# Moving the triangular substitution of a gated DeltaNet layer from SBUF into two PSUM banks

## The chip, the cores and the metric

The kernel runs on one core of a Trainium2 chip. TensorE (PE) multiplies 128 x 128 tiles out of SBUF into PSUM, which has eight banks of 512 float32 columns in 128 partitions; VectorE (DVE), ScalarE (ACT) and GpSimd (POOL) do the elementwise work, and DMA queues are issued from SyncE (SP) and ScalarE. Each engine takes its own instructions in the order of the program and waits for the others on semaphores. The metric is the device time of one execution in microseconds (us); lower is better.

## What is computed

A two-layer encoder trunk over 1024 frames of 1024 features, float32: chunked softmax attention, an MLP, a gated DeltaNet layer, an MLP, a final norm. The change lies in the DeltaNet layer (8 heads of 128). Its core, cut from the reference:

```python
qkv = silu(causal_conv(h @ w_in[:, :3072], conv_w))      # 4 taps; q and k are l2-normalised afterwards
decay = exp(where(incl, gc[..., :, None] - gc[..., None, :], -inf))
L = where(strict, einsum('bhnid,bhnjd->bhnij', k * beta, k) * decay, 0.0)
M = L + eye(CHUNK)
sol = triangular_solve(M, rhs, lower=True, unit_diagonal=True)
...
def step(state, inp):                                    # scan over the chunks of a head
    v_new = u_c - einsum('bhck,bhkv->bhcv', w_c, state)
    o_c = einsum('bhck,bhkv->bhcv', qd_c, state) + einsum('bhij,bhjv->bhiv', qk_c, v_new)
    state = state * gl_c + einsum('bhck,bhcv->bhkv', kd_c, v_new)
    return state, o_c
```

## The kernel before

The kernel computes in chunks of 128 frames, so a head has 8 chunks. Dense products are made with weights and activations split into a high and a low float32r part, three products of 512 columns for each 128 x 128 weight tile; one output tile of 512 columns takes 24 of them and one PSUM bank.

In the DeltaNet stage (`deltanet` and `dn_run`) TensorE works through a list of dense jobs: k for all eight heads, then q, v and z in turn, then the first two panels of the output projection. Everything else is written as generators (tasks). After each dense product `turn` lets those tasks go one step whose priority and whose modelled engine load allow it, so their instructions are woven between the dense products. A model of time (`Clock`) decides in Python which step comes when: it charges an elementwise operation on VectorE about 0.08 us plus its elements at 960 per us, wherever its operands lie. The order that results is the program; on the chip each engine keeps to its own part of it. `Ring` objects model buffers with the modelled time at which each comes free; `sleep` leaves a modelled time for a load, `until` waits for a mark of another task.

The tasks that matter here:

- `dn_evac`: reads a dense bank (`acc`) on VectorE into `xp`, does the four-tap convolution on ScalarE, VectorE and GpSimd with buffers `cy` and `cz`, and writes k, q or v with a Silu on ScalarE. For the k of heads in `POOLED` (4 to 7) one of the additions is made by GpSimd (`cz <- cy, cz`) with a third ScalarE activation; otherwise VectorE makes two scalar_tensor_tensor operations.
- `dn_blocks`: products of k with itself, multiplied by the decays (`U`); the diagonal 32 x 32 blocks go to DRAM (`ud`).
- `dn_solves`: inverts the 32 x 32 diagonal triangles for four heads at a time, so twice (`g` = 0 and 1; "block 1" and "block 2" below), with one triangle in each partition. `fu` is the triangle, scaled with the inverse norms `rt`, which a TensorE transpose and four VectorE copies also spread into `rk`. `Z` (tile `fz`) starts as the identity. 31 steps follow, each a product into `tmp` (tile `ft`) and an addition into `Z`, both tensor_tensor operations on VectorE. `Z` is stored to DRAM as `zd`, and, transposed by ScalarE, as `xd`.
- `dn_inverse`: loads `zd` and `xd` back in another layout (`Zh`, `X`) and puts the inverse of the 128 x 128 triangle together on TensorE.
- `dn_prep_keys`, `dn_prep_queries`, `dn_prep_values`: the other operands, with products through the two `tp` banks.
- `dn_scans`: two lanes (even heads, odd heads) that run the scan over 8 chunks with small products into the PSUM tiles `s1` (two 128 x 128 results) and `s2` (the new state); ScalarE reads the output of a chunk out of `s1` into `o`. Head 0 may begin as soon as its operands are there; the second lane's head 1 waits for block 2.
- `dn_outs`: norm and gate.

PSUM in this stage has two banks for dense results (`acc`), two for `tp`, two for `s1` and two for `s2`. The inner loop of the substitution:

```python
for j in range(31):
    t = tmp[:, : (j + 1) * (31 - j)] ...
    right = Z[:, 0 : j + 1, j + 1 :]
    nc.vector.tensor_tensor(t, Z[:, 0 : j + 1, j : j + 1].broadcast_to(shape), fu[...], ALU.mult)
    nc.vector.tensor_tensor(right, right, t, ALU.add)
    yield
```

In the profile the engine calls of this stage all carry one line, L163 (the wrapper that meters them), so its instructions are told apart by their tiles: `acc`, `xp`, `cy`, `cz`, `fz`, `ft`, `fu`, `tp`, `s` (both scan tiles), `o`.

Of the kernel before, what the change touches and what calls it, by code (L numbers as in the profile page):

```python
# [7 lines left out]
F32 = mybir.dt.float32  # L8
F32R = mybir.dt.float32r
I32 = mybir.dt.int32  # L10
AF = mybir.ActivationFunctionType
ALU = mybir.AluOpType
AX = mybir.AxisListType
PSUM = bass.MemoryType.PSUM
DRAM = bass.MemoryType.DRAM

P = 128
# [3 lines left out]
HB = 512  # L21
# [13 lines left out]
ATT = (3, 2, 0.5, 1, 1, 0.7, 0.6)  # L35
RINGS = {"pt": 2, "po": 2, "sp": 1, "pr": 6, "bias": 3, "thi": 4, "tlo": 3, "oh": 1, "ot": 2}
ENGINES = {"dn_solves": ("vector",), "dn_decays": ("scalar",)}
POOLED = (4, 5, 6, 7)


def wide(col, p, n):
# [4 lines left out]
class Paced:  # L46


    def __init__(self, gens, slots):
        self.gens, self.slots = list(gens), slots  # L50
        self.total, self.done, self.at, self.n = sum(n for _, n in gens), 0, 0, len(gens)
# [13 lines left out]
    def drop(self, first=None):  # L65

        left = 0 if first is None else self.n - first
        while len(self.gens) > left:
            self.step()
# [116 lines left out]
class Ring:  # L186
# [9 lines left out]
    def take(self):  # L196
        if len(self.held) == self.n:
            self.held.pop(0)
        self.held.append([self.new(), None])
        return self.held[-1][0]  # L200

    def give(self, tile, t):
        for h in self.held:
            if h[0] is tile:
                h[1] = t


class Trunk:
# [961 lines left out]
    def up(self, i, ops, ap, mp, pp, gr, gt, finish, A, second, first, tail):  # L1170
# [21 lines left out]
        for n in range(last + 1):  # L1192
# [5 lines left out]
            X = self.bank()  # L1198
            Y, Z = (pp.tile([P, HB], F32, name=self.nm(z), tag=z) for z in "yz")

# [11 lines left out]
            def beside(bit, *steps):  # L1212

                if (G["u_first"] if n == 0 else G["u_second"] if n == 1 else G["u_last"] if n == last else G["u_other"]) >> bit & 1:
                    steps = steps[::-1]
                for step in steps:
                    step()

            def copied(k, ps):
                keep[k] = copy(ps)  # L1220

            def add(k, ps):
                nc.vector.tensor_tensor(keep[k], ps, keep[k], ALU.add)
# [3 lines left out]
            if n == 0:  # L1227
# [9 lines left out]
                next(finish)  # L1237
                self.block_product(Z, A["s1"], ops["t1"], True, True)
                copied("z5", Z)
                add("u2", Z)  # L1240
                R = next(finish)
# [12 lines left out]
            else:  # L1254
                next(sums, None)
                self.block_product(Z, A["s1"], ops["t1"], True, False)
                next(rest, None)
                beside(1, lambda: next(more, None), lambda: copied("z5", Z))
                next(sums, None)
# [414 lines left out]
    def deltanet(self, rhs, finish):  # L1674

        tc = self.tc
        with ExitStack() as es:
            self.tpp = es.enter_context(tc.tile_pool(name="tp", bufs=2, space=PSUM))
            self.sc = es.enter_context(tc.tile_pool(name="sc", bufs=2, space=PSUM))

            self.dq = es.enter_context(tc.tile_pool(name="dq", bufs=1))
            self.d1 = es.enter_context(tc.tile_pool(name="d1", bufs=1))
            self.db = es.enter_context(tc.tile_pool(name="db", bufs=2))
            self.drhs, self.finish = rhs, finish
            self.aux = lambda: self.tpp.tile([P, HB], F32, name=self.nm("tp"), tag="tp")
            rings = {
                "tp": Ring(2, self.aux), "acc": Ring(2, self.bank), "nt": Ring(3, self.nt),
                "s1": Ring(2, lambda: self.sc.tile([P, 2, P], F32, name=self.nm("s1"), tag="s1")),
                "s2": Ring(2, lambda: self.sc.tile([P, P], F32, name=self.nm("s2"), tag="s2"))}
            for t, n in (("xp", 2), ("cy", 2), ("cz", 2)):  # L1690
                rings[t] = Ring(n, lambda t=t, n=n: self.db.tile([P, 64 + HB], F32, name=self.nm(t), tag=t, bufs=n))
            self.begin(rings)
            self.silu_at, self.ready_at, self.solved = 0.0, set(), {}
            return self.timed(self.dn_run)
# [22 lines left out]
    def add(self, priority, steps):  # L1717


        self.tasks.append(Task(priority, steps))  # L1720
        self.tasks.sort(key=lambda t: t.priority)
# [12 lines left out]
    def idle(self):  # L1734

        now = self.clock.now
        self.turn()
        if self.clock.now == now:
            self.clock.at["tensor"] += 0.1
            self.idled += 0.1  # L1740
# [326 lines left out]
    def dn_evac(self, c, h, half, ps):  # L2067
# [17 lines left out]
        else:  # L2085
# [15 lines left out]
            yield  # L2101
            if c == "k" and h in POOLED:
                nc.gpsimd.tensor_tensor(z, y, z, ALU.add)
# [78 lines left out]
    def dn_solves(self):  # L2182

        nc, db = self.nc, self.db
        for g in range(2):
            fu = (self.dq, db)[g].tile([P, 32, 32], F32, name=self.nm("fu"), tag=("kbg", "zT")[g])
            Z = db.tile([P, 32, 32], F32, name=self.nm("fz"), tag="o")
            nc.gpsimd.memset(Z, 0.0)
            nc.gpsimd.memset(Z.rearrange("p c i -> p (c i)")[:, 0 : 32 * 32 : 33], 1.0)
            yield from self.until("u", 4 * g + 3)  # L2190
            nc.sync.dma_start(fu, self.ud[g])
            nb = self.sm.tile([P, 32], F32, name=self.nm("fnb"), tag="fnb")
            v = self.sm.tile([P, 32], F32, name=self.nm("frt"), tag="frt")
            for b in range(4):
                nc.sync.dma_start(
                    nb[32 * b : 32 * b + 32], self.grows[1][32 * g : 32 * g + 32, 32 * b : 32 * b + 32])
            yield from self.sleep(G["sl_solve"])

            diag = fu.rearrange("p j i -> p (j i)")[:, 0 : 32 * 32 : 33]
            nc.vector.tensor_scalar(v, diag, EPS, None, ALU.add)  # L2200
            yield
            yield from self.rsqrt_few(v, 32, "k")
            rt = self.got
            tp = yield from self.take("tp")
            nc.tensor.transpose(tp[:32, :P], rt, self.ident)
            yield
            for b in range(4):
                nc.vector.tensor_copy(
                    self.rk[32 * b : 32 * b + 32, 4 * g : 4 * g + 4].rearrange("p h q -> p (h q)"),
                    tp[:32, 32 * b : 32 * b + 32])  # L2210
            self.give("tp", tp)
            self.mark("rk", g)
            yield
            nc.vector.tensor_tensor(nb, nb, rt, ALU.mult)
            nc.vector.tensor_tensor(
                fu, fu, nb.rearrange("p (o i) -> p o i", o=1).broadcast_to([P, 32, 32]), ALU.mult)
            yield
            nc.vector.tensor_tensor(
                fu, fu, rt.rearrange("p (j o) -> p j o", o=1).broadcast_to([P, 32, 32]), ALU.mult)
            yield  # L2220
            tmp = self.np.tile([P, S], F32, name=self.nm("ft"), tag="ssum")
            for j in range(31):
                shape = [P, j + 1, 31 - j]
                t = tmp[:, : (j + 1) * (31 - j)].rearrange("p (c i) -> p c i", c=j + 1)
                right = Z[:, 0 : j + 1, j + 1 :]
                nc.vector.tensor_tensor(
                    t, Z[:, 0 : j + 1, j : j + 1].broadcast_to(shape), fu[:, j : j + 1, j + 1 :].broadcast_to(shape),
                    ALU.mult)
                nc.vector.tensor_tensor(right, right, t, ALU.add)
                yield  # L2230
            zd = self.dr.tile([P, 32, 32], F32, name=self.nm("zd"))
            xd = self.dr.tile([P, 32, 32], F32, name=self.nm("xd"))
            nc.sync.dma_start(zd, Z)
            X = tmp.rearrange("p (i c) -> p i c", c=32)
            for i in range(2):
                r = slice(16 * i, 16 * i + 16)
                nc.scalar.activation(X[:, r], Z[:, :, r].rearrange("p c i -> p i c"), AF.Copy)
                yield
            nc.scalar.dma_start(xd, X)
            self.solved[g] = zd, xd  # L2240
            self.mark("solve", g)
            yield

    def dn_inverse(self, h):
# [432 lines left out]
```

## Time and profile before

| | before |
|---|---|
| three timed runs | 2543.84, 2547.47, 2551.03 us; median 2547.47 |
| profiled execution | 2544.29 us, span 2542.5 us |
| mean granted TensorE clock | 0.989 of full speed |
| DeltaNet stage in the span | about 1190 to 1820 us |
| substitution, block 1 | 1311.5 to 1370.9 us |
| substitution, block 2 | 1401.8 to 1472.3 us |

The profile counts as busy the time in which an engine executes instructions; the products of TensorE overlap, so a busy TensorE is not necessarily at its peak. Rows that begin with a pair of times such as `1296.00:1382.00` are windows of the span: length, busy time and number of instructions of each engine, granted clock (PEclk), DMA share, GB/s. Rows of a group of instructions give busy time, mean duration in ns, and the idle time of the engine in front of them. A row `A <- B: 7.7, 3, 3.5` says that A waited for B 7.7 us in all, 3 times, at most 3.5 us. A row of the timeline gives start and duration.

### The profile page before, as it was taken

The page shows a single profiled execution, that of the slowest core. Times are in us where ns is not written, and L with a number is a line of the kernel's source. Part 1 is how long each engine was busy: PE and PEld are TensorE (multiplying, and loading weights), DVE is VectorE, ACT ScalarE, POOL GpSimd, SP SyncE. Part 2 cuts the span into 40 slices and gives each one's busy share as a digit, 9 for nine tenths or more (in the row PEclk, how much of TensorE's full clock was granted, in tenths as well). Part 3 has the DMA queues.
Part 4 walks back from the last instruction along what each step waited for, and adds up shares of the span by engine and source line. Part 5 has one row for each costly group of instructions (what it writes and reads, how often), then busy time and mean ns, then how long its engine had stood idle before and what let it go on. Part 6 is the DMA issues. An engine that isn't in the chain of part 4 may idle for free.

```text
span 2542.5 us, 36609 instructions
## 1 busy us (share of the span) xinstructions
PE 2455.7 (97%) x12750; PEld 2047.0 (81%) x12750; DVE 1786.7 (70%) x3058; ACT 1195.2 (47%) x2219; POOL 1287.8 (51%) x1088
## 2 busy tenths in 40 slices
PE   8999999999999999998888999999999999999997
PEld 6888888787888887886777888888787888887886
DVE  6666556678777688887578864444578777678887
ACT  6666667535555433334565333333335555433323
POOL 2444445614666566666474333433414756466655
PEclk9999999999999999999999999999999999999998
DMA  4222223423555977753354221222424555967752
GB/s 159 70 65 72 77 78 115 152 95 141 213 201 211 336 240 265 240 177 116 126 178 131 63 87 66 65 94 86 160 87 145 211 213 200 343 244 253 249 171 83
DMA packets 192760, 398.94 MB, mean 157 GB/s; under 512 B 53232, under 2 KB 59696, under 8 KB 192576
## 3 DMA queue, kind: packets, MB, share of 16 engines
q1 hardware_dynamic: 173136, 352.54, 41.2%
q10 hardware_dynamic: 19440, 44.07, 4.5%
q8 instruction: 100, 1.64, 0.3%
q14 instruction: 84, 0.69, 0.1%
HBM read 257.43 MB, written 130.71 MB: 153 GB/s over the span
## 4 chain that ended last, share of the span: by engine, by line
PE 66%; DVE 8%; issue 2%; DMA 2%; ACT 2%; SPq 1%; POOL 0%; ACTq 0%; DVEq 0%; POOLq 0%
PE y L1013 26%; PE z L1013 12%; PE acc L163 9%; PE acc L1013 7%; PE tp L163 5%; PE s L163 2%; PE acc L277 2%; PE acc L278 2%; PE acc L279 2%; DVE ft L163 1%; DVE fz L163 1%; DVE x L1518 1%; DMA vT<-grows 0%; DVE xs L394 0%; DVE cz L163 0%
## 5 line engine op out<-in xcount | busy, mean ns | idle before, releaser
L163 PE MATMUL acc<-xs,whi 128*128 128x512 f32 x1808 | 632.2, 413 | 13.2 <-DVE xp L163 7.7
L163 PEld LDWEIGHTS acc<-xs,whi 128*128 128x128 f32 x1808 | 335.8, 192 | 69.0 <-issue 4.1
L163 PE MATMUL acc<-xs,wlo 128*128 128x512 f32 x896 | 367.4, 410 | 1.6 <-POOL wlo L163 1.6
L1013 PE MATMUL y<-xs,whi 128*128 128x512 f32 x1008 | 311.7, 390 | 5.2 <-DVE x L1518 1.8
L163 POOL TENSOR_TENSOR wlo<-wraw,whi 128x512 fp32r<-128x512 f32 x126 | 165.8, 1316 | 223.6 <-ACT whi L163 196.0
L1028 POOL TENSOR_TENSOR s<-wraw 128x256 f32<-128x256 f32 (+1 forms) x93 | 92.0, 989 | 350.1 <-DVE a L1019 170.3
L1013 PEld LDWEIGHTS y<-xs,whi 128*128 128x128 f32 x1008 | 188.9, 188 | 47.3 <-DVE x L1518 2.6
L1019 DVE TENSOR_TENSOR wlo<-wraw,whi 128x512 fp32r<-128x512 f32 (+1 forms) x182 | 208.1, 1143 | 25.5 <-ACT whi L1022 25.5
L1022 ACT ACTIVATE whi<-wraw 128x512 fp32r<-128x512 f32 (+2 forms) x191 | 146.4, 767 | 120.4 <-PE y L1013 82.6
L1013 PE MATMUL y<-xs,wlo 128*128 128x512 f32 x504 | 196.4, 390 | 0.1
L1022 ACT ACTIVATE a<-s 128x256 fp32r<-128x256 f32 x122 | 63.8, 524 | 279.9 <-PE y L1013 137.4
L163 PEld LDWEIGHTS acc<-xs,wlo 128*128 128x128 f32 x896 | 172.0, 192 | 28.0 <-POOL wlo L163 2.4
L1013 PE MATMUL y<-xs,a 128*128 128x512 f32 x732 | 187.9, 392 | 6.4 <-DVE x L1518 6.4
L1518 DVE TENSOR_TENSOR x<-y,x 128x512 f32<-128x512 f32 x240 | 165.0, 688 | 34.6 <-PE y L1013 26.7
L1013 PEld LDWEIGHTS y<-xs,a 128*128 128x128 f32 x732 | 136.0, 188 | 40.0 <-DVE x L1518 10.2
L1013 PE MATMUL y<-xs,ahi 128*128 128x512 f32 x512 | 158.7, 391 | 7.7 <-ACT nt L1207 7.7
L1013 PE MATMUL acc<-xs,whi 128*128 128x512 f32 x528 | 162.9, 390 | 0.0
L163 POOL TENSOR_SCALAR pr<-pr,rs 128x640 f32<-128x640 f32 (+4 forms) x128 | 88.1, 691 | 129.4 <-DVE rs L163 98.2
L1013 PE MATMUL z<-xs,whi 128*128 128x512 f32 x480 | 147.9, 389 | 0.0
L163 POOL TENSOR_TENSOR cy<-cy,cz 128x512 f32<-128x512 f32 x48 | 63.0, 1313 | 166.8 <-DVE cz L163 106.6
L1095 DVE TENSOR_TENSOR c<-c 128x512 fp32r<-128x512 f32 x112 | 117.8, 1056 | 31.8 <-POOL c L1025 28.4
L163 DVE CUSTOM_DVE_ANT_0 pr<-sp,bias 128x640 f32<-128x640 f32 (+4 forms) x128 | 83.8, 655 | 64.0 <-PE sp L163 63.0
(351 smaller groups left out, 6087.0 us busy)
## 6 DMA issues: line engine op xcount, KB each, us to landing
xs<-gt SPq DMA_DIRECT2D x256, 256.0 KB, 4.8
gt<-c SPq DMA_DIRECT2D x112, 512.0 KB, 2.9
wraw<-in_w_up_dram SPq DMA_DIRECT2D x64, 512.0 KB, 3.7
wraw<-in_w_down_dram SPq DMA_DIRECT2D x64, 512.0 KB, 4.5
r<-gr SPq DMA_DIRECT2D x88, 256.0 KB, 3.6
wraw<-in_w_in_dram SPq DMA_DIRECT2D x32, 512.0 KB, 3.9
gr<-ssum ACTq DMA_DIRECT2D x62, 256.0 KB, 3.2
wraw<-in_w_qkv_dram SPq DMA_DIRECT2D x30, 512.0 KB, 3.4
```

Source lines behind the costliest of these rows:

```text
L163: return call(*args, **more)
L277: nc.tensor.matmul(ps, hi[:, k], xh, start=(k == 0), stop=False)
L278: nc.tensor.matmul(ps, hi[:, k], xl, start=False, stop=False)
L279: nc.tensor.matmul(ps, lo[:, k], xh, start=False, stop=(k == KT - 1))
L1013: nc.tensor.matmul(ps, w[:, k], x, start=bool(first and f), stop=bool(last and e), skip_group_check=True)
L1019: self.nc.vector.tensor_tensor(lo, src, hi.bitcast(F32), ALU.subtract)
L1022: self.nc.scalar.activation(hi, src, AF.Copy)
L1028: self.nc.gpsimd.tensor_tensor(out, x, y, ALU.add)
L1095: nc.vector.tensor_tensor(t[z][:, HB:].bitcast(F32R), t[z][:, HB:], t[z][:, :HB], ALU.subtract)
L1518: nc.vector.tensor_tensor(x, ps, x, ALU.add)
```

## The change

- The PSUM pool of the scans has one bank for `s1` and one for `s2`, and a tile `zz` of two banks.
- Until block 1 begins, the second bank of `zz` is a third bank for dense results (class `Spare`; `drop` takes it away once it is idle).
- `Z` is `zz`. It is filled by VectorE instead of GpSimd, after the loads of `fu` have been issued; the 9 us of `sl_solve` are counted from the same point as before.
- `rk` is written by one VectorE transpose of 32 x 32 blocks instead of a TensorE transpose and four copies.
- At the end ScalarE copies `zz` into an SBUF tile `F` (`fz`), and ScalarE's queue stores it; before, SP's queue stored `Z`. The transposed copies read `zz`.
- After block 2 the two banks become the second `s1` and `s2`.
- `POOLED` is empty.

```diff
-POOLED = (4, 5, 6, 7)
+POOLED = ()
...
+class Spare(Ring):
+    def __init__(self, n, new, spare=None):
+        super().__init__(n + (spare is not None), new)
+        self.spare = spare
+
+    def take(self):
+        spare = self.spare is not None and len(self.held) == self.n - 1
+        if len(self.held) == self.n:
+            spare = self.held.pop(0)[0] is self.spare
+        self.held.append([self.spare if spare else self.new(), None])
+        return self.held[-1][0]
+
+    def idle(self, now):
+        return all(t is not None and t <= now for x, t in self.held if x is self.spare)
+
+    def drop(self):
+        self.held = [x for x in self.held if x[0] is not self.spare]
+        self.n -= 1
+        self.spare = None
+
+    def add(self, spare):
+        self.n += 1
+        self.spare = spare
...
-            self.sc = es.enter_context(tc.tile_pool(name="sc", bufs=2, space=PSUM))
+            self.sc = es.enter_context(tc.tile_pool(name="sc", bufs=1, space=PSUM))
+            self.zz = self.sc.tile([P, 2, HB], F32, name="zz")
...
-                "tp": Ring(2, self.aux), "acc": Ring(2, self.bank), "nt": Ring(3, self.nt),
-                "s1": Ring(2, lambda: self.sc.tile([P, 2, P], F32, name=self.nm("s1"), tag="s1")),
-                "s2": Ring(2, lambda: self.sc.tile([P, P], F32, name=self.nm("s2"), tag="s2"))}
+                "tp": Ring(2, self.aux), "acc": Spare(2, self.bank, self.zz[:, 1]), "nt": Ring(3, self.nt),
+                "s1": Spare(1, lambda: self.sc.tile([P, 2, P], F32, name=self.nm("s1"), tag="s1")),
+                "s2": Spare(1, lambda: self.sc.tile([P, P], F32, name=self.nm("s2"), tag="s2"))}
...  (dn_solves)
-            Z = db.tile([P, 32, 32], F32, name=self.nm("fz"), tag="o")
-            nc.gpsimd.memset(Z, 0.0)
-            nc.gpsimd.memset(Z.rearrange("p c i -> p (c i)")[:, 0 : 32 * 32 : 33], 1.0)
+            zz = self.zz.rearrange("p b n -> p (b n)")
+            Z = zz.rearrange("p (c i) -> p c i", i=32)
...
-            yield from self.sleep(G["sl_solve"])
+            begin = self.clock.now
+            if g == 0:
+                while not self.rings["acc"].idle(self.clock.now):
+                    yield
+                self.rings["acc"].drop()
+            nc.vector.memset(zz, 0.0)
+            nc.vector.memset(zz[:, 0 : 32 * 32 : 33], 1.0)
+            yield
+            yield from self.sleep(begin + G["sl_solve"] - self.clock.now)
...
-            tp = yield from self.take("tp")
-            nc.tensor.transpose(tp[:32, :P], rt, self.ident)
-            yield
-            for b in range(4):
-                nc.vector.tensor_copy(
-                    self.rk[32 * b : 32 * b + 32, 4 * g : 4 * g + 4].rearrange("p h q -> p (h q)"),
-                    tp[:32, 32 * b : 32 * b + 32])
-            self.give("tp", tp)
+            nc.vector.transpose(self.rk[:, 4 * g : 4 * g + 4].rearrange("p h q -> p (h q)"), rt)
...
-            nc.sync.dma_start(zd, Z)
+            F = db.tile([P, 2, HB], F32, name=self.nm("fz"), tag="o")
+            for i in range(2):
+                nc.scalar.activation(F[:, i], self.zz[:, i], AF.Copy)
+                yield
+            nc.scalar.dma_start(zd, F.rearrange("p b (c i) -> p (b c) i", i=32))
...
             self.mark("solve", g)
+            if g:
+                self.rings["s1"].add(self.zz[:, 0, : 2 * P].rearrange("p (n t) -> p n t", t=P))
+                self.rings["s2"].add(self.zz[:, 1, :P])
             yield
```

## The prediction

> **What bounds the kernel now.** I read the page first: engine shares, then the slices with the granted clock.
>
> ```profile
> span 2542.5 us, 36609 instructions
> PE 2455.7 (97%) x12750; PEld 2047.0 (81%) x12750; DVE 1786.7 (70%) x3058; ACT 1195.2 (47%) x2219; POOL 1287.8 (51%) x1088
> ```
>
> TensorE is busy 97% of the span, so this change can only return time in which TensorE stands still, or runs at a lowered clock, in the DeltaNet stage. I cut that stage into windows to see how much there is.
>
> ```profile
> core 0: us, PE busy (x) PEld busy (x) DVE busy (x) ACT busy (x) POOL busy (x), PEclk, DMA share, GB/s
> 1214.00:1296.00 82.00, 76.30 (x355) 62.49 (x356) 44.20 (x92) 53.06 (x93) 42.67 (x32) 0.96 0.48 152
> 1296.00:1382.00 86.00, 69.65 (x346) 56.07 (x345) 79.14 (x130) 48.37 (x88) 49.88 (x41) 0.92 0.45 142
> 1382.00:1400.00 18.00, 18.00 (x154) 14.57 (x154) 13.48 (x32) 8.13 (x16) 6.97 (x7) 1.00 0.52 160
> 1400.00:1484.00 84.00, 79.96 (x682) 67.63 (x680) 71.99 (x147) 29.82 (x59) 28.75 (x23) 0.96 0.20 62
> 1484.00:1800.00 316.00, 314.34 (x2182) 271.07 (x2181) 157.09 (x361) 114.31 (x228) 114.83 (x84) 0.99 0.27 87
> ```
>
> A window loses its length less PE busy, and on top of that (1 - PEclk) of its length. From 1296 to 1382, where the first substitution runs, that is 16.4 us idle and 0.08 x 86 = 6.9 us of clock: 23.2 us. From 1400 to 1484, the second substitution: 4.0 and 3.4, so 7.4 us. From 1214 to 1296: 5.7 and 3.3, so 9.0 us. Behind 1484 TensorE is idle for only 1.7 us of 316. VectorE fills 79.14 of 86 us in the worst window; the chain of waits says whose work that is, and the waits of TensorE say what it stood for.
>
> ```profile
> by line: DVE ft L163 20.5%; DVE fz L163 19.4%; issue 12.8%; DVE cz L163 6.3%; DVE xp L163 5.9%; DMA vT<-grows 5.5%; DVE U L163 5.1%; DMA xd<-ft 3.8%; PE acc L163 2.9%; DVE fu L163 2.7%; DVE cy L163 2.5%; PE tp L163 2.5%; DMA X<-xd 2.3%; ACT
> PE acc L163 <- DVE xp L163: 7.7, 3, 3.5
> PE tp L163 <- ACT nt L163: 3.2, 2, 2.2
> PE tp L163 <- ACT k L163: 2.8, 2, 1.7
> PE tp L163 <- DMA X<-xd: 1.3, 2, 0.9
> ```
>
> In this window (all five rows are for 1296 to 1382) 40% of the chain is the substitution's two operations, `ft` (product) and `fz` (addition). TensorE waits 7.7 us for `xp`, the reading of a dense bank, which queues behind them on VectorE.
>
> **The change, part by part.** (a) *Z in PSUM.* Each block runs 31 steps of two tensor_tensor operations on (j+1)(31-j) elements, 5456 elements in all for each of the two. What they take, block 1 and then block 2:
>
> ```profile
> L163 DVE TENSOR_TENSOR fz<-fz,ft 128x31 f32<-128x31 f32 (+15 forms) x31 | 24.3, 784 | 1.1
> L163 DVE TENSOR_TENSOR ft<-fz,fu 128x31 f32<-128x31 f32 (+15 forms) x31 | 19.3, 624 | 0.5
> L163 DVE TENSOR_TENSOR ft<-fz,fu 128x31 f32<-128x31 f32 (+15 forms) x31 | 20.7, 668 | 0.2
> L163 DVE TENSOR_TENSOR fz<-fz,ft 128x31 f32<-128x31 f32 (+15 forms) x31 | 17.1, 551 | 1.1
> ```
>
> So 43.6 and 37.8 us. The timeline shows what undisturbed ones take, and what disturbs them:
>
> ```profile
> 1341.35 0.43 DVE L163 TENSOR_TENSOR fz<-fz,ft 128x256 f32<-128x256 f32 x1
> 1401.75 0.19 DVE L163 TENSOR_TENSOR ft<-fz,fu 128x31 f32<-128x31 f32 x1
> ...
> 1460.38 1.04 POOL L163 TENSOR_TENSOR ub<-ub,rk 64x512 f32<-64x512 f32 x1
> 1460.50 4.16 DVE L163 TENSOR_TENSOR ft<-fz,fu 128x112 f32<-128x112 f32 x1
> 1461.39 1.89 POOL L163 TENSOR_TENSOR dc<-dc,rk 128x1024 f32<-128x1024 f32 x1
> 1463.24 1.28 POOL L163 TENSOR_TENSOR wlo<-wraw,whi 128x512 fp32r<-128x512 f32 x1
> 1464.69 0.27 DVE L163 TENSOR_TENSOR fz<-fz,ft 128x112 f32<-128x112 f32 x1
> ```
>
> 0.43 us for 256 elements and 0.19 for 31 give 0.155 us plus 1/960 us an element. Hence 62 x 0.155 + 2 x 5456/960 = 21.0 us a block undisturbed: 22.6 and 16.8 us are stretching. The `ft` of 112 elements that lasted 4.16 us began inside one GpSimd operation and ended with the third of a row of them; its twin took 0.27. Is it the two SBUF inputs? Operations of this stage with one input in PSUM, and ones with both in SBUF (ns, min/median/max):
>
> ```profile
> L163 DVE TENSOR_TENSOR xp<-acc,R x48: 672/683/694, 1216.3 to 1752.1; 128x512 f32<-128x512 f32 x48
> L163 DVE SCALAR_TENSOR_TENSOR cz<-xp,convw,cz x48: 737/744/1780, 1218.4 to 1754.4; 128x512 f32<-128x512 f32 x48
> L163 DVE SCALAR_TENSOR_TENSOR cy<-xp,convw,cy x40: 737/747/2285, 1217.7 to 1753.7; 128x512 f32<-128x512 f32 x40
> ```
>
> With a PSUM input the 48 spread over 22 ns; with two SBUF inputs single ones reach 1780 and 2285. Since Z now supplies one input of both operations, the stretching goes: -22.6 and -16.8 us of VectorE. A PSUM source itself costs nothing: 683 ns at 512 elements against 0.155 + 512/960 = 0.688 by the SBUF fit. What no row shows is VectorE writing PSUM, which `fz` now does in place. Bounds: if reading and writing one bank took turns, 5456/960 = 5.7 us more a block; if a PSUM result were quicker by the 34 ns that separate ScalarE's 597 (PSUM source, below) from its 631 (SBUF source), 31 x 0.034 = 1.1 us less. I take 0, the nearest row being the `xp` one.
>
> [...]
>
> (b) *Filling Z.* GpSimd loses two memsets a block; VectorE gets them. Bounds for the large one: 0.96 us (GpSimd's own, below) to 1.22 (VectorE's 1024-element `fu`, below); with the strided one of 32, +1.4 us a block on VectorE. They stand inside the 9 us sleep that covers the loads of `fu`; without that cover they would add 1.4 us to the chain.
>
> (c) *rk by one VectorE transpose.* A TensorE transpose, 0.45 us of waiting and four copies (0.77 us) become one 32-column operation, bounded by 0.18 (one such copy) and 0.4: about -0.5 us of VectorE and -1.0 us of chain a block, one `tp` bank less in use.
>
> (d) *POOLED empty.* For heads 4 to 7, so 8 halves: GpSimd loses an addition (1318 ns), ScalarE an activation (715 ns), VectorE gains a scalar_tensor_tensor (0.745 undisturbed). Six of the eight additions lie in the worst window: +4.5 us of VectorE there, -7.9 us of GpSimd.
>
> (e) *Z's way out.* ScalarE copies two halves (597 ns each by the `vb` row) and issues the store that SP issued at once; X's two strided copies (1156 ns each) follow, from PSUM, for which no row has a stride: between 597 and 1156 each, and I take 1156. The X chain behind the substitution starts 1.2 us later, and its 1.3 us wait (`X<-xd`) grows by up to that: +1 us a block. SP loses a 0.34 us issue with the Z loads of the inverse behind it; ScalarE's queue gains one, with the X copies behind it.
>
> ```profile
> 1304.04 0.77 DVE L163 COPY rk<-tp 32x32 f32<-32x32 f32 x4 [0.45 <-PE tp L163]
> L163 POOL TENSOR_TENSOR cz<-cy,cz 128x512 f32<-128x512 f32 x8 | 10.5, 1318 | 0.9 <-ACT cz L163 0.9
> L163 ACT ACTIVATE cy<-xp,convw 128x512 f32<-128x512 f32 x36 | 25.6, 715 | 23.3 <-DVE xp L163 20.8 <-POOL cz L163 2.4
> L163 ACT ACTIVATE ft<-fz 128x512 f32<-128x512 f32 x4 | 4.5, 1156 | 5.9 <-DVE fz L163 5.9
> L163 DVE TENSOR_TENSOR fu<-fu,ry 128x1024 f32<-128x1024 f32 x2 | 2.4, 1222 | 0.0
> L163 ACT ACTIVATE vb<-tp 128x512 f32<-128x512 f32 x4 | 2.4, 597 | 4.0 <-PE tp L163 4.0
> L163 POOL MEMSET fz<- 128x1024 f32 x1 | 1.0, 963 | 0.0
> 1370.95 0.34 SPq L2233 DMA_DIRECT2D zd<-fz  x1
> L163 ACT ACTIVATE k<-cy 128x512 f32<-128x512 f32 x16 | 10.1, 631 | 14.2 <-POOL cy L163 13.8
> L163 ACT ACTIVATE o<-s x8: 277/277/278, 1409.4 to 1456.1; 128x128 f32<-128x128 f32 x8
> ```
>
> (f) *Third dense bank until block 1.* From 1214 to 1296 TensorE's waits are these, none for a dense bank to be read; I count 0.
>
> ```profile
> PE tp L163 <- DVE U L163: 2.6, 2, 2.0
> PE tp L163 <- DVE qT L163: 1.7, 1, 1.7
> ```
>
> The others are under 1 us each (`wlo`, `R`, `kn`). The wait for the bank to fall idle lies in the same sleep.
>
> (g) *One bank of each kind for head 0's scan.* The `o<-s` row above is that scan: eight chunks in 46.7 us, while block 2 still runs. The next chunk's first product now waits for the 277 ns eviction that a second bank hid; dense products fill in between, so I count +1 us, from 0 to 7 x 0.28 = 2.
>
> **The sum.** VectorE in the worst window falls from 79.1 by 22.6 and 0.5, and gains 1.4 and 4.5: 62 of 86 us, 72%. In the second window it falls from 72.0 to about 56 of 84, 67%. What does TensorE lose at such a load? The rows above: 9.0 of 82 us at 54%, nothing of 18 at 75%, 7.4 of 84 at 86%. Nearest are the last two; I take the dearer one, so 7.6 of 86 us in the first window: 23.2 - 7.6 = 15.6 us back. In the second I take half of 7.4: 3.7. Against that (e) 2 and (g) 1, and 1.3 for things that the new order of the whole stage puts together less well. Net -15 us. Behind 1484 TensorE has no slack in which this could be lost or made up, so it reaches the end. The profiled execution took 2544.3 us; the three runs are 2543.8, 2547.5, 2551.0, so it is a fast one, 3.2 under their median. 2544.3 - 15 = 2529.3; beside the median, 2532.
>
> **The rivals.**
> *More comes back* (2520). The lost time of 1214 to 1296 also shrinks, through the third bank and GpSimd's relief, and the second window recovers fully: 9.0 x 0.8 + 3.7 = 11 more. Against it: no dense bank is waited for there. Chance 0.17.
> *Little comes back* (2541). The order in which TensorE's work is interleaved is written anew; products wait for `cz`, `cy` and the rsqrt operations, which keep two SBUF inputs, and six more such join the worst window. If `xp` comes no earlier than these let it, only the three `xp` waits (7.7 us) go and the clock stays: -6. Against it: 40% of the chain there is `ft` and `fz`. Chance 0.17.
> *PSUM writes are slow* (2538). If in-place addition takes two turns an element, VectorE regains 11.4 us of 39.4, and 15 us becomes about 9. Nothing speaks for it but the missing row. [...] Chance 0.10 for both.
> *Slower, by the single scan bank* (2556). If head 0's products are placed on TensorE where ScalarE is still behind with the solve's copies (2 x 0.6 + 2 x 1.16 = 3.5 us), TensorE, which takes its work in order, stops for up to that at each of 7 chunks: +24, net +9. It decides from 2.1 us a chunk (15/7). For it: the scan and block 2 overlap. Against: the copies come once, at the block's end. Chance 0.10 with everything else that ends slower.
>
> **How the numbers follow.** My forecast (2523 to 2539) has 0.46; with the rivals 0.17, 0.17, 0.10 and 0.10. A measurement of this kernel tells about 0.3% (7.6 us) from no change, so faster means below 2539.8: 0.46 + 0.17 + most of the slow-PSUM case (0.06) = 0.69; the same 0.21, slower 0.10. The range runs from 2514 to 2550: it takes in the larger return with its spread, and both small-return cases up to no change; about 0.08 lies above, 0.07 below.
>
> **What would show it.** Right: the 62 operations of a block sum to 20 to 23 us with none above 0.6; block 1 takes some 40 us instead of 60; PE idle in its window falls below 9 us, the clock rises to 0.95 or more; the `xp` waits of TensorE are under 3 us. (b): a 1.0 to 1.3 us memset on VectorE. Wrong: operations on Z near twice their size, stretched `cz` and `cy` in their place, TensorE waiting on `s` for ScalarE, or a stage that is as long although VectorE is emptier, which would put the bound into the order and not into VectorE.

## The result and the profile after

The changed kernel takes 2529.55 us (median of four runs, 2528.32 to 2530.82) where the kernel before took 2547.86 beside it: a ratio of 0.9932, with a 95% interval of 0.9920 to 0.9944. The forecast was 2532, in a range of 2514 to 2550. The profiled execution has a span of 2526.2 us. The medians and ratios below leave out two slow executions, 2656 and 6282 us, of the run with Z back in SBUF, whose other ten took 2538 to 2548.

The page's first lines, then the same windows as before:

```profile
span 2526.2 us, 36563 instructions
PE 2446.5 (97%) x12748; PEld 2041.2 (81%) x12748; DVE 1765.3 (70%) x3064; ACT 1194.2 (47%) x2217; POOL 1275.8 (51%) x1076
...
core 0: us, PE busy (x) PEld busy (x) DVE busy (x) ACT busy (x) POOL busy (x), PEclk, DMA share, GB/s
1214.00:1296.00 82.00, 71.81 (x337) 58.87 (x336) 45.21 (x94) 50.77 (x90) 36.83 (x28) 0.96 0.43 143
1296.00:1382.00 86.00, 75.13 (x434) 61.87 (x433) 69.82 (x146) 51.56 (x93) 48.33 (x37) 0.96 0.58 174
1382.00:1400.00 18.00, 18.00 (x148) 15.20 (x147) 15.00 (x36) 8.97 (x16) 8.21 (x7) 1.00 0.20 50
1400.00:1484.00 84.00, 82.46 (x720) 70.74 (x719) 58.14 (x143) 30.67 (x64) 30.23 (x25) 1.00 0.29 92
...
1484.00:1780.00 296.00, 296.00 (x2052) 254.28 (x2051) 149.75 (x337) 109.69 (x217) 108.02 (x78) 0.99 0.26 83
```

Length less PE busy, plus (1 - PEclk) of the length, is what a window loses. The first substitution's window now loses 10.9 + 3.4 = 14.3 us (23.2 before), the second's 1.5 (7.4 before). The window ahead of them loses more: 10.2 + 3.3 = 13.5 (9.0 before). The last row ends at 1780, since the end of the stage, with its own idle time, has moved forward by some 17 us. A window holds other work in the two kernels, so these numbers give the pattern and not a balance. The whole span gives one: TensorE's idle time falls from 86.8 to 79.7 us, so by 7.1, and the mean granted clock rises from 0.989 to 0.992, which by the same rule is 7 to 8 us. Together that is some 15 of the 16.3 us between the two spans, about half of it clock.

The substitution itself, all 124 operations (ns, min/median/max), then block 1 alone in groups (busy us, mean ns):

```profile
L163 DVE TENSOR_TENSOR ft<-zz,fu x62: 176/358/423, 1319.5 to 1453.4; 128x31 f32<-128x31 f32 x4, 128x60 f32<-128x60 f32 x4, 128x87 f32<-128x87 f32 x4, 128x112 f32<-128x112 f32 x4
L163 DVE TENSOR_TENSOR zz<-zz,ft x62: 198/366/433, 1319.7 to 1453.6; 128x31 f32<-128x31 f32 x4, 128x60 f32<-128x60 f32 x4, 128x87 f32<-128x87 f32 x4, 128x112 f32<-128x112 f32 x4
...
L163 DVE TENSOR_TENSOR zz<-zz,ft 128x31 f32<-128x31 f32 (+15 forms) x31 | 10.8, 349 | 1.1
L163 DVE TENSOR_TENSOR ft<-zz,fu 128x31 f32<-128x31 f32 (+15 forms) x31 | 10.4, 336 | 0.6
```

The longest of them lasts 0.433 us, where single ones lasted over 4 us before. A block sums to 21.2 us, from 43.6 and 37.8. Block 1 runs from 1319.5 to 1363.9 (44.4 us, before 59.4), block 2 from 1392.5 to 1453.9 (61.4 us, before 70.5). What TensorE still waits for, 1214 to 1484:

```profile
PE acc L163 <- DVE xp L163: 4.7, 1, 4.7
PE tp L163 <- DVE qT L163: 4.4, 1, 4.4
PE tp L163 <- DVE U L163: 3.4, 3, 2.0
PE zz L163 <- POOL wlo L163: 2.3, 1, 2.3
...
PE s L163 <- DVE ft L163: 1.5, 1, 1.5
```

The `xp` wait is one, not three; the wait of 4.4 us for `qT` (the gates, from 1229) was 1.7 us before.

### The profile page after: what moved, and what is told of

It reads as the page before. It is cut to its first block, busy times and chain, and to the rows that moved or that the text cites. A ratio compares the mean times of both kernels' runs of the same rounds, so it can differ in the third digit from the quotient of the medians.

```text
span 2526.2 us, 36563 instructions
## 1 busy us (share of the span) xinstructions
PE 2446.5 (97%) x12748; PEld 2041.2 (81%) x12748; DVE 1765.3 (70%) x3064; ACT 1194.2 (47%) x2217; POOL 1275.8 (51%) x1076
## 4 chain that ended last, share of the span: by engine, by line
PE 68%; DVE 6%; DMA 2%; issue 2%; ACT 2%; POOL 1%; SPq 0%; ACTq 0%; DVEq 0%; POOLq 0%
PE y L1040 26%; PE z L1040 12%; PE acc L163 11%; PE acc L1040 7%; PE tp L163 5%; PE acc L306 2%; PE acc L305 2%; PE acc L304 2%; PE s L163 1%; PE zz L163 1%; DVE x L1545 1%; DMA row<-grows 1%; DVE xs L421 0%; DVE cy L163 0%; DMA xs<-gt 0%
## 5 line engine op out<-in xcount | busy, mean ns | idle before, releaser
L163 PE MATMUL acc<-xs,whi 128*128 128x512 f32 x1744 | 606.9, 410 | 9.7 <-DVE xp L163 4.7
L163 PEld LDWEIGHTS acc<-xs,whi 128*128 128x128 f32 x1744 | 321.4, 190 | 61.8 <-ACT whi L163 4.9
L163 PE MATMUL acc<-xs,wlo 128*128 128x512 f32 x864 | 352.2, 408 | 1.7 <-POOL wlo L163 1.7
L163 PEld LDWEIGHTS acc<-xs,wlo 128*128 128x128 f32 x864 | 164.5, 190 | 25.9 <-POOL wlo L163 2.1
L1040 PE MATMUL acc<-xs,whi 128*128 128x512 f32 x528 | 162.9, 390 | 0.0
```

The costliest lines, as they stand in the source:

```text
L163: return call(*args, **more)
L1040: nc.tensor.matmul(ps, w[:, k], x, start=bool(first and f), stop=bool(last and e), skip_group_check=True)
```

## The experiments

Theory A: the gain comes from the place of Z alone, because an operation with two SBUF inputs stands still while GpSimd reads SBUF. Rival B: it comes from the new order of the stage (third dense bank, POOLED, `rk`). The median of the kernel before lies between 2545.7 and 2546.9 us beside the runs below.

**Z back in SBUF, same order.** Every engine has the same operations in the same order as in the changed kernel; only where Z lies differs.

```diff
-            zz = self.zz.rearrange("p b n -> p (b n)")
+            own = db.tile([P, 2, HB], F32, name=self.nm("fz"), tag="o")
+            zz = own.rearrange("p b n -> p (b n)")
...
-                nc.scalar.activation(F[:, i], self.zz[:, i], AF.Copy)
+                nc.scalar.activation(self.zz[:, i], own[:, i], AF.Copy)
...
-            nc.scalar.dma_start(zd, F.rearrange("p b (c i) -> p (b c) i", i=32))
+            nc.scalar.dma_start(zd, Z)
```

> The changed kernel with Z back in SBUF: the same instructions in the same order on all engines (the two ScalarE copies still write the PSUM tile, the store takes Z itself); only the place of Z differs. Theory A (with two SBUF inputs the substitution stands still while GpSimd reads): each block's 62 operations sum to 36 to 45 us instead of 21, the window of the first substitution loses 20 us or more of TensorE time again, and the time goes back to 2543 (2538 to 2548). Rival B (the gain is that of the new order: third dense bank, POOLED, rk): the operations may stretch, but the time stays within 2527 to 2533.

Measured 2542.78 us (median of ten), ratio to before 0.9985 (0.9976 to 0.9994). The window of the first substitution and the two operations over both blocks:

```profile
1296.00:1382.00 86.00, 71.91 (x324) 58.75 (x323) 73.88 (x130) 49.25 (x86) 43.90 (x33) 0.90 0.48 148
...
L163 DVE TENSOR_TENSOR fz<-fz,ft 128x31 f32<-128x31 f32 (+15 forms) x62 | 41.3, 666 | 2.1
L163 DVE TENSOR_TENSOR ft<-fz,fu 128x31 f32<-128x31 f32 (+15 forms) x62 | 34.1, 550 | 0.9
...
PE acc L163 <- DVE xp L163: 9.0, 4, 3.9
```

37.7 us a block, 14.1 + 8.6 = 22.7 us lost in the window, TensorE waiting for `xp` four times. So some 13 of the 18 us are the place of Z; all the other edits together, with the order that they bring, are worth about 4.

**The product in PSUM, Z in SBUF, same order.** As above, with the product tile in the two banks:

```diff
+            prod = self.zz.rearrange("p b n -> p (b n)")
-                t = tmp[:, : (j + 1) * (31 - j)].rearrange(...)
+                t = prod[:, : (j + 1) * (31 - j)].rearrange(...)
```

> As the run before (Z in SBUF, same order), but the product is written into PSUM: the multiplication then has two SBUF inputs and a PSUM result, the addition one input of each kind and an SBUF result. Theory A says it is the inputs: the additions are undisturbed (31 of them sum to 10.5 us a block, none above 0.6 us), the multiplications stretch (18 to 25 us a block), and about half of the loss of the run before comes back: 2536 (2532 to 2541). If an SBUF result is what collides, it is the other way round: additions stretch, multiplications do not.

Measured 2535.12 us, ratio 0.9958 (0.9946 to 0.9970).

```profile
L163 DVE TENSOR_TENSOR zz<-fz,fu 128x31 f32<-128x31 f32 (+15 forms) x62 | 38.5, 621 | 0.9
L163 DVE TENSOR_TENSOR fz<-fz,zz 128x31 f32<-128x31 f32 (+15 forms) x62 | 21.0, 338 | 2.1
```

The operation with two SBUF inputs stretches (19.3 us a block, result in PSUM); the one with one input in PSUM does not (10.5 us, result in SBUF). It is the inputs, and half of the cure brings a little over half of the gain, 7.7 of 13 us.

**GpSimd without reads.** Z in SBUF, same order; GpSimd's two-input operations in the DeltaNet stage are replaced by fills:

```diff
+            if self.name == "gpsimd" and op == "tensor_tensor" and self.clock.fills:
+                out = args[0].bitcast(F32) if args[0].dtype == F32R else args[0]
+                return self.real.memset(out, ...)
```

> The changed kernel with Z in SBUF, in the same order, and with every two-input operation of GpSimd in the DeltaNet stage replaced by a fill of its output (zeros, or -1e30 for the masked decays), which reads no SBUF; so the DeltaNet result is left out. If theory A is right in naming GpSimd's reading as the other party, the substitution runs undisturbed although Z lies in SBUF: 62 operations in 20 to 23 us a block, none above 0.7. If something else of the SBUF side delays them (DMA writes, ScalarE, TensorE's reading), they stretch as in the run with Z in SBUF, to 33 to 42 us a block. The total time falls too, since fills are shorter; it is not compared.

```profile
L167 DVE TENSOR_TENSOR ft<-fz,fu x62: 177/359/426, 1315.3 to 1442.3; 128x31 f32<-128x31 f32 x4, 128x60 f32<-128x60 f32 x4, 128x87 f32<-128x87 f32 x4, 128x112 f32<-128x112 f32 x4
L167 DVE TENSOR_TENSOR fz<-fz,ft x62: 191/359/425, 1315.6 to 1442.5; 128x31 f32<-128x31 f32 x4, 128x60 f32<-128x60 f32 x4, 128x87 f32<-128x87 f32 x4, 128x112 f32<-128x112 f32 x4
...
L167 DVE TENSOR_TENSOR fz<-fz,ft 128x31 f32<-128x31 f32 (+15 forms) x62 | 21.3, 343 | 2.1
L167 DVE TENSOR_TENSOR ft<-fz,fu 128x31 f32<-128x31 f32 (+15 forms) x62 | 20.9, 338 | 0.9
L166 POOL MEMSET wlo<- 128x512 f32 x22 | 11.3, 522 | 32.5 <-PE acc L167 32.5
```

21.1 us a block and nothing above 0.43 us, with Z in SBUF and GpSimd still writing (busy 19.2 of the 86 us from 1296 to 1382, in the changed kernel 48.3). With that the other party of a two-input operation is named: GpSimd's reads. The fills are shorter than what they replace (522 ns instead of some 1300), so less GpSimd time is there to collide with; but not one of the 124 operations is stretched, and the 96 `cy` and `cz` operations of the stage average 0.747 and 0.745 us. (Its single execution took 2516.55 us; fills are shorter, so the time says nothing.) This run, the one before (19.3 us a block with two SBUF inputs, 10.5 with one) and the 21.2 us of the changed kernel agree.

**The order before, Z alone in PSUM.** The kernel before with its own order; Z's memset, its copies out and the banks of the scans are put in without the model knowing, so nothing else moves:

```diff
+            nc.real.vector.memset(zz, 0.0)          # nc.real: not charged in the model
+            nc.real.vector.memset(zz[:, 0 : 32 * 32 : 33], 1.0)
...
-            nc.sync.dma_start(zd, Z)
+            for i in range(2):
+                nc.real.scalar.activation(F[:, i], self.zz[:, i], AF.Copy)
+            nc.real.scalar.dma_start(zd, F.rearrange("p b (c i) -> p (b c) i", i=32))
```

> The kernel before, in its own order, with Z alone moved to the two PSUM banks: VectorE fills Z behind the loads, ScalarE copies it out and stores it, the scans have one bank of each kind until block 2 is done; no third dense bank, POOLED and rk as before. Theory A: the 62 operations of a block sum to 21 us and most of the gain is there: 2534 (2529 to 2538). Rival B: within 2543 to 2550. The single scan bank, if it is dear, shows as TensorE waiting at s for ScalarE from 1400 to 1475, more than 2 us in all.

Measured 2532.51 us, ratio 0.9939 (0.9927 to 0.9951): -14.4 us from the other side, in an order made by a model that charges both places alike. Of the single scan bank, which head 0 has while block 2 runs, TensorE's waits from 1400 to 1475 show this much:

```profile
PE zz L163 <- ACT ft L163: 1.5, 1, 1.5
PE tp L163 <- DVE ov L163: 0.6, 1, 0.6
```

The 1.5 us are not a wait for the eviction of the single bank, which the prediction's (g) counted: no such wait is in the rows. At 1462, with block 2 done, the scan gets `zz` as its second bank while ScalarE is still making the transposed copy out of it. The rival of +24 us needed a wait for these copies at each of 7 chunks; it came once. In the changed kernel the one wait from 1400 to 1475 is the 1.5 us of `s` in the rows above: the state that TensorE needs stands on VectorE behind a `cy` that lasted 3.61 us.

**The other edits, one by one.** The third dense bank taken out of the changed kernel:

```diff
-                "tp": Ring(2, self.aux), "acc": Spare(2, self.bank, self.zz[:, 1]), "nt": Ring(3, self.nt),
+                "tp": Ring(2, self.aux), "acc": Ring(2, self.bank), "nt": Ring(3, self.nt),
...
-            if g == 0:
-                while not self.rings["acc"].idle(self.clock.now):
-                    yield
-                self.rings["acc"].drop()
```

> The changed kernel without the third dense bank (its order is written anew from the first DeltaNet products on). Prediction's step (f): the bank is worth 0, 2530 (2526 to 2534). Rival: the bank is worth 5 us or more, 2535 and above. It also tells whether the 10 us of idle TensorE time from 1214 to 1296 in the changed kernel (5.7 before) come with the third bank.

Measured 2528.23 us (0.9925, 0.9912 to 0.9938). No worth of the bank shows. The wait for `qT` is back at 1.7 us without it, as in every kernel here with two dense banks; every one with three has 4.4. From 1214 to 1296 TensorE is idle for 8.1 us, between the 5.7 of before and the 10.2 with the bank.

POOLED as before, in the changed kernel:

```diff
-POOLED = ()
+POOLED = (4, 5, 6, 7)
```

> The changed kernel with POOLED as before, (4, 5, 6, 7); the order is written anew. Theory A, with the prediction's step (d) (4.5 us of VectorE in the worst window, not its bound any more): 2530 (2525 to 2535). If emptying POOLED carried a good part of the gain: 2536 or more.

Measured 2525.33 us (0.9917, 0.9903 to 0.9931): 4 us below the changed kernel, but the intervals overlap. And `rk` as before, in the changed kernel:

```diff
-            nc.vector.transpose(self.rk[:, 4 * g : 4 * g + 4].rearrange("p h q -> p (h q)"), rt)
+            tp = yield from self.take("tp")
+            nc.tensor.transpose(tp[:32, :P], rt, self.ident)
+            yield
+            for b in range(4):
+                nc.vector.tensor_copy(
+                    self.rk[32 * b : 32 * b + 32, 4 * g : 4 * g + 4].rearrange("p h q -> p (h q)"),
+                    tp[:32, 32 * b : 32 * b + 32])
+            self.give("tp", tp)
```

> The changed kernel with rk by a TensorE transpose and four copies, as before; the order is written anew from block 1 on. Prediction's step (c): worth 0.5 us of VectorE and 1 us of chain a block: 2530 (2527 to 2535). A rival in which the start of the substitution is what counts: 2535 or more.

Measured 2527.40 us (0.9928, 0.9915 to 0.9941). POOLED emptied in the kernel before:

```diff
-POOLED = (4, 5, 6, 7)
+POOLED = ()
```

> The kernel before with POOLED empty, nothing else; the order is written anew. Prediction's step (d) beside stretched operations: VectorE, 92% full in the worst window, gets 4.5 us more there: 2550 (2546 to 2555). If relief of GpSimd is what counts (fewer reads to collide with, -10.5 us of GpSimd), it is faster: 2535 to 2543.

Measured 2545.99 us, ratio 1.0007 (0.9995 to 1.0019): no change, neither the loss nor the gain that was expected. The substitution is stretched to 34.6 us a block there (40.7 before), perhaps by 8 additions fewer on GpSimd, perhaps by the new order, and the window loses about what it lost (22.1 us):

```profile
1296.00:1382.00 86.00, 72.52 (x334) 60.03 (x333) 78.34 (x136) 43.28 (x75) 44.07 (x35) 0.90 0.49 153
```

**Combinations, on one chip.** Each puts several of these edits together in the changed kernel.

> The changed kernel with POOLED as before and without the third dense bank. If the edits beside Z add up as they did one by one against the changed kernel (2529.6): 2525.3 for POOLED, 2528.2 for the bank, so 2524 (2519 to 2530). If each of them only moves the order to another with its own idle moments, they do not add: 2526 to 2534.

> The changed kernel with POOLED and rk as before. Additive: 2525.3 and 2527.4 against 2529.6 give 2523 (2519 to 2528). Not additive: 2526 to 2532.

> The kernel before with Z in PSUM and its banks alone, the order written anew with the memset on VectorE and the copies out of PSUM in the model (third bank, POOLED and rk as before). Theory A: Z's place carries all of the gain, so no slower than the whole change: 2525 (2520 to 2533). A rival in which the other edits carry 5 us or more: 2535 and above.

> The changed kernel beside the three others on one chip: 2529.6 as before (2527 to 2532); it is here so that a difference of a few us to them is read on one chip.

| kernel | median us | ratio to before (95%) |
|---|---|---|
| the changed kernel again | 2528.06 | 0.9931 (0.9919 to 0.9944) |
| POOLED as before, two dense banks | 2516.92 | 0.9890 (0.9876 to 0.9903) |
| POOLED and `rk` as before | 2527.76 | 0.9934 (0.9921 to 0.9946) |
| POOLED, `rk` and dense banks as before: Z alone | 2521.29 | 0.9914 (0.9899 to 0.9928) |

By the medians the edits do not add: POOLED and `rk` taken back together bring 0 instead of -6, POOLED and the bank -11 instead of -6, below both ranges expected. The fastest of all keeps Z in PSUM and `rk` by VectorE, and drops the two other edits. Its first window:

```profile
1296.00:1382.00 86.00, 80.51 (x476) 65.69 (x475) 73.08 (x157) 58.44 (x107) 53.08 (x42) 0.96 0.53 171
```

5.5 + 3.4 = 8.9 us lost, where the changed kernel loses 14.3. TensorE waits for `xp` nowhere from 1214 to 1484 there. Why this order fits so well is not shown; each of the four is another weaving of the same work. Z alone lies 6.8 us below the whole change, with intervals that just overlap (0.9928 and 0.9919). That speaks for the order and not for the price of an edit, since single ones taken back bring 1 to 4, but no run separates the two.

## Why the prediction was right, and where it was not

- *(a), the size and the cause.* 22.6 and 16.8 us of stretching were to go; 22.4 and 16.6 went (43.6 and 37.8 to 21.2). In-place addition in PSUM, for which no row stood, costs next to nothing: 10.8 us a block, against 10.5 when the additions write SBUF. No run shows in-place additions that take two turns an element, nor more than 8 ns of surcharge on operations that read PSUM: the smallest product took 176 ns and the smallest addition 198 with an input in PSUM, 177 and 191 with both in SBUF in the run without GpSimd's reads; the longest took 423 and 433, there 426 and 425.
- *The sum.* -15 us forecast; -18.3 by the medians, -14.4 and about -13 when the place of Z is isolated from either side. That it came out so close is partly luck, since the terms per window are off in both directions. First window: 7.6 us were to be left, 14.3 are. Second window: 3.7 were to be left, 1.5 are. The window ahead of them was to stay at 9.0 and loses 13.5. The step that failed is taking the loss from windows of like VectorE load. The forecast's own rows already showed no such order (9.0 us lost at 54%, nothing at 75%, 7.4 at 86%), and of the runs the one with VectorE busy 73.1 us in the first window loses 8.9, the changed kernel with 69.8 loses 14.3. (The forecast had 62 us there.) What counts is which operation TensorE waits for. Its longest wait, 4.7 us for `xp`, looks like this:

```profile
1305.49 2.48 POOL L163 TENSOR_TENSOR vT<-vT,mask 128x512 f32<-128x512 f32 x2 [2.91 <-DMA vT<-grows]
1305.66 1.14 DVE L163 TENSOR_SCALAR ry<-rt 128x32 int32<-128x32 int32 x1
1306.83 1.20 DVE L163 TENSOR_TENSOR ru<-ry 128x32 f32<-128x32 f32 x1
1308.07 1.19 DVE L163 SCALAR_TENSOR_TENSOR ru<-ru,frt 128x32 f32<-128x32 f32 x1
1309.29 1.19 DVE L163 SCALAR_TENSOR_TENSOR ru<-ru 128x32 f32<-128x32 f32 x1
1310.41 0.68 DVE L163 TENSOR_TENSOR xp<-acc,R 128x512 f32<-128x512 f32 x1
1311.23 1.19 PE L163 MATMUL acc<-xs,whi 128*128 128x512 f32 x2 [4.69 <-DVE xp L163]
...
1312.06 0.19 DVE L163 TENSOR_TENSOR ru<-ry 128x32 f32<-128x32 f32 x1
```

  Four small operations for the inverse norms, whose inputs still lie in SBUF, last 1.1 to 1.2 us each, as long as the GpSimd operations beside them, where 0.19 is the undisturbed time; the reading of the bank stands behind them. In the run without GpSimd's reads, which has the same order, `ru<-ry` averages 0.17 us and TensorE is idle for 2.4 us of that window instead of 10.9. So stretching that is left on other operations, not VectorE's load, makes the longest wait.
- *The signs named beforehand.* The operations on Z and the clock in the window (0.96) came as said. Block 1 took 44.4 us instead of some 40, TensorE's idle time in its window is 10.9 us instead of under 9, and the `xp` wait 4.7 instead of under 3.
- *(f)* was counted at 0 because no dense bank was waited for. In time it is 0, but the step failed in its mechanism: with a third bank in the model the products around the gates' transposes are placed otherwise, and TensorE stands 4.4 us for `qT` instead of 1.7.
- *(b)* 0.91 + 0.09 us a block on VectorE (1.4 forecast; the large memset lies just below its bounds). *(c)* the transpose took 0.21 us, inside the bounds. *(e)* was too dear: the transposed copies out of PSUM take half of what they took from SBUF, so the four copies of a block cost what the two did, and TensorE's 1.3 us wait for X (`X<-xd`), which was to grow, is gone in the changed kernel. *(g)* +1 us was counted for the evictions of the single bank; no wait for one is seen.

```profile
L163 DVE MEMSET zz<- 128x1024 f32 x2 | 1.8, 912 | 0.4 <-DVE U L163 0.2 <-DVE xp L163 0.2
L163 DVE STREAM_TRANSPOSE rk<-ry 128x32 f32<-128x32 f32 x2 | 0.4, 211 | 0.1
L163 ACT ACTIVATE ft<-zz 128x512 f32<-128x512 f32 x4 | 2.4, 590 | 0.4 <-ACT fz L163 0.4
L163 ACT ACTIVATE fz<-zz 128x512 f32<-128x512 f32 x4 | 2.3, 594 | 4.3 <-DVE zz L163 4.2
```

- *(d)* +4.5 us of VectorE were to be paid in the worst window. Emptying POOLED costs nothing in the kernel before; in the changed one the medians say 4 us, which the intervals leave open. In the changed kernel the convolution's operations, which still have two SBUF inputs, meet GpSimd. From 1290 to 1470, the kernel before and then the changed one:

```profile
L163 DVE SCALAR_TENSOR_TENSOR cz<-xp,convw,cz 128x512 f32<-128x512 f32 x18 | 13.4, 744 | 4.0 <-POOL cz L163 4.0
L163 DVE SCALAR_TENSOR_TENSOR cy<-xp,convw,cy 128x512 f32<-128x512 f32 x12 | 10.5, 874 | 1.3 <-ACT cy L163 1.3
...
L163 DVE SCALAR_TENSOR_TENSOR cy<-xp,convw,cy 128x512 f32<-128x512 f32 x18 | 18.2, 1010 | 10.3 <-ACT cy L163 9.3 <-POOL vT L163 1.0
L163 DVE SCALAR_TENSOR_TENSOR cz<-xp,convw,cz 128x512 f32<-128x512 f32 x18 | 16.5, 917 | 0.0
```

  Beside 0.745 us undisturbed that is 1.5 us too much before (30 operations) and 7.9 after (36). So some 6 of the 39 us of stretching moved from the substitution to them, as the rival "little comes back" had it; it was too small to decide.

## What to carry to other kernels

Compare the longest with the shortest duration of one form of operation. Where small VectorE operations with two SBUF inputs last as long as the GpSimd operations beside them, one input in PSUM took the delay away here (a block of 43.6 and one of 37.8 us became 21.2), and the same order of instructions with only that tile's place changed shows it without any other effect (37.7 us a block with Z in SBUF). Expect a part of the delay to move to the operations that keep both inputs in SBUF (here some 6 of 39 us), and look which of them TensorE waits for. And when several edits go in at once and the order of a stage is written anew, test each back out: here the place of Z was most of the gain, and with two of the edits beside it taken back the kernel is 11 us faster.

## What the runs showed of the hardware that was not expected

- ScalarE's copy with a transposed read (stride 32) took 1156 ns from SBUF and 590 from PSUM, as much as a plain copy from PSUM (594). With Z in SBUF and without GpSimd's reads it took 1121, so those reads are not the cause; what is, was not tried.
- Operations with one SBUF input are not all spared. The copies of three columns `xp<-xp` take 0.16 us, but single ones last 1.6 us in the changed kernel and still 0.96 in the run without GpSimd's reads (second row), where none of the 124 operations on Z lasted over 0.43. Where GpSimd only writes, something of the delay is left for these; what, was not tried.

```profile
L163 DVE COPY xp<-xp x24: 153/164/1615, 1216.5 to 1731.3; 128x3 f32<-128x3 f32 x24
L167 DVE COPY xp<-xp x24: 153/162/958, 1220.9 to 1722.8; 128x3 f32<-128x3 f32 x24
```

- The granted clock varies between runs of one kernel, and the time with it: without the third bank 2521.99 us at 0.991 and 2533.02 at 0.987; 0.004 of 2530 us is 10 of the 11 us between them. In the latter, profiled one the clock was at half from about 1378 to 1398 (0.50 in each window of 4 us from 1380 to 1396; a single product of 512 columns lasted 0.63 us there, 0.39 before it) although TensorE's rows fill that time. In front of it TensorE stood still for 2.77 us, waiting for the X of the inverse, and again for 0.42:

```profile
1376.69 0.66 PE L163 MATMUL tp<-X,ua 32*32 32x32 f32 x16 [2.77 <-DMA X<-xd]
1377.77 1.06 PE L163 MATMUL tp<-X,ua 32*32 32x32 f32 x16 [0.42 <-DMA X<-xd]
...
1380.00:1384.00 4.00, 4.00 (x40) 3.20 (x40) 2.94 (x9) 1.85 (x3) 0.00 (x0) 0.50 0.36 82
...
1392.00:1396.00 4.00, 4.00 (x23) 3.35 (x24) 1.09 (x4) 0.00 (x0) 0.00 (x0) 0.50 0.00 0
```

What brought the half rate on, and why it lasted some 20 us, is not shown. Some of the products in it are of 32 x 32 and of one column; whether that plays a part was not tried.
